# A two-branch attention layer on one core: exponentials of the second attention copied by ScalarE's queue into fp32r buffers and transposed there, over 15-row key ranges

## The chip, the cores and the metric

The kernel runs on one NeuronCore of a Trainium2 chip. The metric is device microseconds (us) from start to end of the program, the median of three runs. A profile of one further execution gives the start and duration of every instruction on the core's five engines: PE (TensorE; its weight loads are listed as PEld), DVE (VectorE), ACT (ScalarE), POOL (GpSimd) and SP (SyncE, which here issues almost all DMAs). Less than 0.2% (5 us) cannot be told from no change.

## The reference

Two sequences of 2048 tokens, width 1024, go through one layer with shared weights:

```
h = rms_norm(x)
q_a,k_a,v_a,g_a,q_b,k_b,v_b,g_b = split(h @ w_in)
A: 8 query heads, 2 key heads, keys within +-128 tokens, rotary, a learned sink per head
B: tokens as a grid of 32 rows x 64 columns; 8 heads; a query sees 8 rows x 16 columns of keys:
   rs = clip(row - 4, 0, 24);  cs = clip(col - 8, 0, 48)
   pr = softmax(q.k / 8 + relative position bias);  o = pr @ v
x = x + concat(o_a * silu(g_a), o_b * silu(g_b)) @ w_out
y = x + (p @ w_ple) * sigmoid(x @ w_ple_gate)
```

Everything is float32, head dimension 64. The second attention, B, is what the change touches.

## The kernel before, in words

**Arithmetic.** Matmul operands have the type fp32r, 4 bytes wide like fp32, which an engine that writes it rounds. To keep accuracy an operand is split in two fp32r parts, high (a cast on ACT) and low (the rest, by DVE or POOL), and a product takes three matmuls. Transposes go through PE too: the data is the stationary operand (it is loaded by LDWEIGHTS), an identity matrix of 128 columns streams past it, and the result appears in PSUM. They work on plain fp32 data with an fp32 identity (`ident`, or `rowwise`, which also permutes the tokens of a block).

**Stages.** Start: inputs and the first weights are loaded and split. Stage A (to about 780 us): projections of 32 blocks of 128 tokens (`proj_a`), with the first attention (`unit_a`) between their matmuls. Stage B (about 800 to 1815 us): projections for the second attention (`proj_b`; 24 matmuls `pqk` and 24 `pvg` per block and half of the heads), 64 of them, with 64 units of attention (`unit_b`) between. From about 1815 us on: the products with `w_out`, `w_ple_gate` and `w_ple` (a little of `w_ple` is done in the last units, `ple_ahead`).

**A unit of B.** A unit is one block of 8 x 16 queries and four heads. Its key window is `window(b, cb)`: `nr` rows of `ncol` columns, cut in chunks of `rows` rows, so that a chunk has at most 128 keys. The windows are 12 x 24, 12 x 32, 15 x 24 and 16 x 32 (rows x columns). The actions of a unit are:

- `sc(h)`, for h = 0 to 3: two matmuls into the PSUM tile `scb`; DVE adds the bias and takes the row maximum (`s`, `mx`).
- `exp`: ACT replaces each `s` by its exponentials, heads in the order 0, 2, 1, 3; the loads of the values `vw` are issued.
- `fin`, of the unit before (transposes `pgtb`), and `prep` (queries of the next unit, transposes `pqtb`).
- `pt(x)`: three or four transposes `ptb` of one head's exponentials; ACT and DVE split them into `p_t`.
- `po(x)`: three or four matmuls `pob` with the values; two by two they are added up by ACT and DVE (`otb`).

**What sets the order.** All PE instructions stand in the order in which the code gives them (`pinned`). `PLAN_B` says at which share of a unit's projection matmuls an action is put between them: a row (0.45, 1, "pt", 0) puts the first transposes of this unit behind 45% of them; a 0 in second place means the unit before. The other engines' instructions, and all DMAs, are ordered by a scheduler, except those that `P` keeps in the order of the code and those that `behind` ties to a matmul. Each queue is strictly in order, SP's and ACT's too. A DMA adds to one of eight completion counters (DMAHW0 to 7), taken in turn by all DMAs of SP and ACT, and waits until the DMA eight places before it has landed.

**Memory.** The 128 partitions' memory is given out by pools of tagged buffers. The tag `ev` has three buffers of 640 floats: in stage A for pairs of scores, at the end of stage B for results of `ple_ahead`; between, it is unused.

Of the kernel before, what the change touches and what calls it, by code (L numbers as in the profile page):

```python
# [11 lines left out]
F32 = mybir.dt.float32  # L12
F32R = mybir.dt.float32r
# [6 lines left out]
NT = SEQ // 128  # L20
# [2 lines left out]
NEG = -1.0e30  # L23
EPS = 1e-6

ROW_WIN = {0: (0, 12, 12), 1: (4, 16, 15), 2: (12, 16, 15), 3: (20, 12, 12)}
COL_WIN = {0: (0, 24), 1: (8, 32), 2: (24, 32), 3: (40, 24)}


def window(b, cb):  # L30
    c0, nc_ = COL_WIN[cb]
    r0, wide, narrow = ROW_WIN[b]
    nr = wide if nc_ == 32 else narrow
    rows = 5 if nr == 15 else 4
    return r0, nr, c0, nc_, rows


def row_type(b):
# [6 lines left out]

def query_rows(b, cb, j):

    r0, _, _, _, rows = window(b, cb)
    k0 = r0 + rows * j
    see = [r for r in range(8) if k0 - 7 <= min(max(8 * b + r - 4, 0), 24) <= k0 + rows - 1]  # L50
    return (see[0], max(see[-1] + 1, 4)) if see[0] == 0 else (min(see[0], 4), see[-1] + 1)


def bias_offsets():
# [28 lines left out]
TW = 512  # L83
# [10 lines left out]
PLAN_B = (  # L94
    (0.00, 1, "sc", 0), (0.03, 1, "sc", 1), (0.07, 1, "sc", 2), (0.09, 0, "po", 2), (0.11, 1, "sc", 3), (0.16, 0, "po", 3),
    (0.16, 1, "exp", 0), (0.24, 0, "fin", 0), (0.35, 1, "prep", 0),
    (0.45, 1, "pt", 0), (0.52, 1, "pt", 1), (0.60, 1, "pt", 2), (0.66, 1, "po", 0), (0.74, 1, "pt", 3), (0.80, 1, "po", 1),
)


def emit(ctx, tc, io):
# [6 lines left out]
        tag = PSM.get(tag, tag)  # L108
        return pp.tile(shape, F32, tag=tag, name=name, bufs=PSB[tag])

    ident = cp.tile([128, 128], F32, tag="ident", name="ident")
    make_identity(nc, ident)

    rowwise = cp.tile([128, 128], F32, tag="rowwise", name="rowwise")
    nc.gpsimd.tensor_copy(rowwise.rearrange("p (r c) -> p r c", c=16), ident.rearrange("p (c r) -> p r c", r=8))
    nw = cp.tile([128, KT], F32, tag="nw", name="nw")
    nc.scalar.dma_start(nw, io["norm_w"])
    ms_a = cp.tile([128, 2 * NT], F32, tag="ms_a", name="ms_a")
# [118 lines left out]
    def pinned(ins):  # L237

        if last_pe:
            tc.add_manual_dep(ins.ins, last_pe.pop().name,  # L240
                              mybir.DependencyInfo(mybir.DependencyClass.NoSync, mybir.DependencyReason.DATA),
                              reason="tensor engine order")
        last_pe.append(ins.ins)
# [8 lines left out]
        pinned(nc.tensor.matmul(out, lhsT, rhs, start=start, stop=stop))  # L252

    def tr(out, in_, eye=ident):
        pinned(nc.tensor.transpose(out, in_, eye))  # L255

    def project(ps, xr, w, cost):

# [16 lines left out]
    def exps(sm, fct, gs, sink=None):  # L275

        mx, nm, den, rd, ss = (sm[k] for k in ("mx", "nm", "den", "rd", "s"))
        if sink is None:
            nc.vector.tensor_scalar_mul(nm, mx, -1.0)  # L279
            yield  # L280
        else:
            nc.vector.scalar_tensor_tensor(out=nm, in0=mx, scalar=-1.0, in1=sink[1], op0=ALU.mult, op1=ALU.min)
        for n_, i in enumerate((0, 2, 1, 3) if sink is None else range(4)):
            ex = nc.scalar.activation(ss[i], ss[i], AF.Exp, bias=nm[:, i:i + 1], accum_out=den[:, i:i + 1])  # L284
# [374 lines left out]
        qrest[f] = split_q(pqt, q1, q2, 1)  # L659
        return q1, q2  # L660

    p_rot = []

    def unit_a(f, kv):
        s, t = divmod(f, NT)
# [5 lines left out]
        def sc(i):  # L671
            pair, half = divmod(i, 2)
            a, z = span[half]
            c0, n = 128 * t - 128 + 64 * half, z - a
            if half == 0:
                pairs.append(ap.tile([128, 640], F32, tag="ev", name="s2", bufs=3))
# [168 lines left out]
    def unit_b(f):  # L845
# [2 lines left out]
        b, cb = divmod(j, 4)  # L848
        _, gs = held[f]
        r0, nr, c0, ncol, rows = window(b, cb)  # L850
        kc, nch = rows * ncol, nr // rows
        n = nr * ncol
        if cb != 2:
            off, _ = BIAS_OFF[(row_type(b), col_type(cb))]
# [7 lines left out]
        def load_values():  # L862

            spare = f >= 6 * NT - 6 and f % 2 == 0
            if spare:
                four = ap.tile([128, 4, 4, 2 * HD], F32R, tag="raw", name="vw4", bufs=1)
            for j in range(nch):
                v = four[:, j] if spare else \
                    ap.tile([128, 4, 2 * HD], F32R, tag=("vp", "vr_")[j % 2], name="vw", bufs=3 - j % 2)
                nc.sync.dma_start(v[:kc].bitcast(F32).rearrange("p h d -> p (h d)"),  # L870
                                  v_d[half, s, cb][r0 + rows * j:r0 + rows * j + rows]
                                  .rearrange("r c h a d -> (r c) (h a d)"))
                vw.append(v)

# [5 lines left out]
        def sc(h):  # L880
            ps = ptile([128, 512], "sc", "scb")
            for j, q in enumerate(qs[f]):
                mm(ps[:, :n].rearrange("p (r c) -> p r c", c=ncol), q[h % 2][:, 128 * (h // 2):128 * (h // 2) + 128],
                   ks_b[h % 2][:, r0:r0 + nr, h // 2, c0:c0 + ncol], j == 0, j == 1)
            softmax(h, ps, n, bias[:, h, :n], sm)
            if h == 3:
                got["ex"] = exps(sm, hr_b[:, st:st + 1], gs)
                next(got["ex"])

        def pt(x):  # L890
            h = (0, 2, 1, 3)[x]
            pt = ptile([128, 512], "pt", "ptb")
            for j in order:

                c = at[j] - 16 * sees[j][0]
                tr(pt[:kc, c:c + 128], sm["s"][h][:, kc * j:kc * j + kc], rowwise)
# [3 lines left out]
            nc.vector.tensor_tensor(out=lo, in0=pf, in1=hi.bitcast(F32), op=ALU.subtract)  # L900
            p_ts.append(p_t)

        def po(x):
            h = (0, 2, 1, 3)[x]
            e, i = h % 2, h // 2
            if i == 0:
                got["po"] = ptile([128, 2, 256], "ms", "pob")
            if x == 0:
                got["ot"] = ap.tile([128, 2, 2, 128], F32, tag="ot", name="otb", bufs=2)
            po, ot = got["po"], got["ot"]  # L910
            for j in order[::-1]:
                a, z = sees[j]
                mm(po[:, i, :].rearrange("p (a q) -> p a q", a=2)[:, :, 16 * a:16 * z], vw[j][:kc, h, :],
                   p_ts[x][:kc, :, at[j]:at[j + 1]], j == order[-1], j == order[0])
            if i == 1:
                a, z = 64 * e, 64 - 64 * e
                pq = po.rearrange("p i (a q) -> p i a q", a=2)
                nc.scalar.copy(ot[a:a + 64], pq[z:z + 64])  # L918
                nc.vector.tensor_tensor(out=ot[a:a + 64], in0=pq[a:a + 64], in1=ot[a:a + 64], op=ALU.add)  # L919
# [58 lines left out]
            early[name].append(w)  # L978
        del coming[:n]

    made = []

    def store_ple(n):

# [4 lines left out]
    def ple_ahead(n, tail=False):  # L989

        load_p(n + 1)
        for m in range(KT):
# [11 lines left out]
            if tail:  # L1004
                ev = main.tile([128, TW], F32, tag="s", name="ev", bufs=SB)
            else:
                ev = ap.tile([128, TW], F32, tag=("ev", "sq")[m // 2 % 2], name="ev", bufs=3 - m // 2 % 2)
            P(nc.scalar.copy(ev, ps))
            store_ple(1)
            if tail:  # L1010
# [416 lines left out]
```

## Time and profile before

| | |
|---|---|
| Three runs, us | 2465.88, 2467.28, 2467.45; median 2467.28 |
| Span of the profiled execution, first to last instruction, us | 2462.8 |
| Busy, share of the span | PE 100%, PEld 84%, DVE 69%, ACT 57%, POOL 35% |
| Granted TensorE clock | 1.000 of full speed |
| DMA traffic | 442.01 MB, 179 GB/s on average |

The profiled execution is a run of its own; the page gives its span, which is 4.5 us under the median of the three runs. Its time outside the span is not listed, so those 4.5 us are taken as what lies around the span.

How to read it: PE counts as busy whenever a matmul is in its pipeline, and matmuls overlap there, so 100% says that PE is always occupied, not that it runs at its best rate. The rate is seen in the chain that ended last, which gives each piece the time by which it delays the next. In lists of groups, "128*96 128x128" behind a PE instruction means 128 rows by 96 columns of stationary data, and 128 columns that stream past.

### The profile page before, as it was taken

To read this page: it belongs to the slowest core of one execution; us is meant where nothing else is said; L and a number is where in the kernel's file an instruction comes from. 1 tells how busy PE (TensorE), PEld (TensorE's weight loads), DVE (VectorE), ACT (ScalarE), POOL (GpSimd) and SP (SyncE) were. 2 spreads that over 40 slices of the span, in tenths; PEclk is the share of its full clock that TensorE was granted. 3 is DMA by queue.
4 is the path that set the end of the run, shared out by engine and by line. 5 is a ranking of instruction groups with operands and counts; after the bars stand their busy time and mean duration, and the time that the engine had idled before them with its cause. 6 is when DMAs were issued, how large, how long until landed. Compare 5 with 4: busy or idle time off the path is not lost.

```text
span 2462.8 us, 40532 instructions
## 1 busy us (share of the span) xinstructions
PE 2451.7 (100%) x13062; PEld 2075.4 (84%) x13062; DVE 1704.7 (69%) x4214; ACT 1413.1 (57%) x3408; POOL 856.8 (35%) x1363
## 2 busy tenths in 40 slices
PE   9999999999999999999999999999999999999999
PEld 8888888888888888888888888888888888888887
DVE  7777777777765666666666666666537655677776
ACT  6777776777664665656655566665763222344433
POOL 4555555555543544454444444443100000000000
PEclk9999999999999999999999999999999999999999
DMA  6332223332255565556955566667977445856765
GB/s 228 123 103 93 95 89 103 95 101 88 95 180 166 167 192 182 183 163 195 314 187 183 170 219 202 193 199 242 317 248 262 154 165 178 270 180 206 251 222 171
DMA packets 243316, 442.01 MB, mean 179 GB/s; under 512 B 27904, under 2 KB 82592, under 8 KB 237856
## 3 DMA queue, kind: packets, MB, share of 16 engines
q1 hardware_dynamic: 242816, 439.42, 54.8%
q8 instruction: 104, 1.70, 0.3%
q14 instruction: 108, 0.88, 0.1%
q10 hardware_dynamic: 288, 0.01, 0.0%
HBM read 309.29 MB, written 134.23 MB: 180 GB/s over the span
## 4 chain that ended last, share of the span: by engine, by line
PE 94%; DVE 2%; ACT 2%; POOL 1%; issue 1%; DMA 1%; SPq 0%; ACTq 0%; POOLq 0%; DVEq 0%
PE pvg L252 15%; PE pqk L252 14%; PE acca L1230 14%; PE accc L1230 11%; PE pg L252 6%; PE pq L252 6%; PE scb L252 4%; PE ptb L255 4%; PE pple L252 4%; PE pob L252 3%; PE po L252 3%; PE pk L252 3%; PE sc L252 3%; PE pt L255 2%; DVE pr L712 1%
## 5 line engine op out<-in xcount | busy, mean ns | idle before, releaser
L284 ACT ACTIVATE s<-s,nm 128x320 f32<-128x320 f32 (+6 forms) x512 | 294.5, 576 | 318.5 <-DVE nm L279 198.9
L252 PE MATMUL pvg<-wb,xr 128*128 128x512 f32 x1536 | 461.5, 407 | 0.0
L252 PE MATMUL pqk<-wa,xr 128*128 128x512 f32 x1536 | 442.9, 411 | 0.0
L252 PEld LDWEIGHTS pqk<-wa,xr 128*128 128x128 f32 x1536 | 266.1, 189 | 36.7
L252 PEld LDWEIGHTS pvg<-wb,xr 128*128 128x128 f32 x1536 | 266.8, 189 | 30.8
L1212 ACT CAST opd<-raw 128x512 fp32r<-128x512 f32 x224 | 131.5, 618 | 271.7 <-PE acca L1230 118.0
L353 POOL TENSOR_TENSOR xr<-stx,xr 128x512 fp32r<-128x512 f32 x186 | 238.9, 1295 | 101.3 <-ACT xr L352 76.8
L1213 DVE TENSOR_TENSOR opd<-raw,opd 128x512 fp32r<-128x512 f32 x224 | 146.7, 687 | 146.9 <-ACT opd L1212 146.9
L252 PE MATMUL pg<-wb,xr 128*128 128x512 f32 x768 | 233.3, 410 | 1.0 <-DVE vv L510 1.0
L252 PE MATMUL pq<-wa,xr 128*128 128x512 f32 x768 | 219.3, 400 | 0.0
L268 DVE CUSTOM_DVE_ANT_0 s<-scb,bias 128x288 f32<-128x288 f32 (+3 forms) x256 | 142.2, 556 | 104.6 <-PE scb L252 101.7
L137 POOL TENSOR_TENSOR yb<-vrb,power 128x8 f32<-128x8 f32 x64 | 106.4, 1662 | 222.1 <-DVE vrb L784 202.4
L1230 PE MATMUL accc<-opd,wb 128*128 128x512 f32 x768 | 176.7, 389 | 0.0
L1230 PE MATMUL acca<-opd,wa 128*128 128x512 f32 (+1 forms) x780 | 175.9, 386 | 0.5 <-ACT r L1308 0.5
L1230 PE MATMUL acca<-opd,s 128*128 128x512 f32 x768 | 175.4, 389 | 0.0
L1230 PEld LDWEIGHTS acca<-opd,wa 128*128 128x128 f32 x780 | 145.0, 188 | 30.2 <-ACT r L1308 0.7
L1230 PEld LDWEIGHTS acca<-opd,s 128*128 128x128 f32 x768 | 144.2, 188 | 29.9
L1230 PEld LDWEIGHTS accc<-opd,wb 128*128 128x128 f32 x768 | 144.2, 188 | 29.9
L919 DVE TENSOR_TENSOR otb<-pob,otb 64x512 f32<-64x512 f32 x128 | 88.1, 688 | 113.2 <-ACT otb L918 111.5
L252 PEld LDWEIGHTS pob<-p_t,vw 128*128 128x128 f32 (+2 forms) x832 | 132.6, 189 | 23.4 <-DVE p_t L900 3.4
L252 PEld LDWEIGHTS pq<-wa,xr 128*128 128x128 f32 x768 | 135.2, 189 | 17.3
L712 DVE TENSOR_TENSOR pr<-pt,pr 128x512 fp32r<-128x512 f32 (+2 forms) x248 | 135.4, 549 | 15.9 <-ACT pr L710 12.5
(171 smaller groups left out, 5169.9 us busy)
## 6 DMA issues: line engine op xcount, KB each, us to landing
stx<-x_b SPq DMA_DIRECT2D x128, 256.0 KB
vw<-v_d SPq DMA_DIRECT2D x112, 256.0 KB
stx<-x_a SPq DMA_DIRECT2D x64, 256.0 KB
stn<-x_n SPq DMA_DIRECT2D x64, 256.0 KB
v_d<-vb SPq DMA_DIRECT2D x64, 256.0 KB
ple_d<-ev SPq DMA_DIRECT2D x64, 256.0 KB
xres<-x_r SPq DMA_DIRECT2D x64, 256.0 KB
x_d<-r SPq DMA_DIRECT2D x64, 256.0 KB
```

The source lines that it names most:

```text
L137: nc.gpsimd.tensor_tensor(out=y, in0=v, in1=power.broadcast_to([128, n]), op=ALU.pow)
L252: pinned(nc.tensor.matmul(out, lhsT, rhs, start=start, stop=stop))
L255: pinned(nc.tensor.transpose(out, in_, eye))
L268: nc.vector.tensor_tensor_reduce(out=s, in0=ps[:, :n], in1=bias, scale=1.0, scalar=-3.0e38, op0=ALU.add, op1=ALU.max, accum_out=sm["mx"][: ...
L284: ex = nc.scalar.activation(ss[i], ss[i], AF.Exp, bias=nm[:, i:i + 1], accum_out=den[:, i:i + 1])
L353: low.tensor_tensor(out=lo, in0=raw, in1=hi.bitcast(F32), op=ALU.subtract)
L712: nc.vector.tensor_tensor(out=pr[r, 1, to], in0=pt[r, c], in1=pr[r, 0, to].bitcast(F32), op=ALU.subtract)
L919: nc.vector.tensor_tensor(out=ot[a:a + 64], in0=pq[a:a + 64], in1=ot[a:a + 64], op=ALU.add)
L1212: P(nc.scalar.copy(hi, v))
L1213: P(nc.vector.tensor_tensor(out=lo, in0=v, in1=hi.bitcast(F32), op=ALU.subtract))
L1230: pinned(nc.tensor.matmul(ps[:, cols], w[k][:, a, c:c + 128], o[:, b, cols], start=i in (0, 1, 4) and k == 0 and j == 0, stop=k == 3 and j ...
```

## The change

Four things, all of which concern stage B, its buffers or its identities:

1. **Key ranges.** The windows of 16 x 32 become 15 x 32 (8 query rows see no more than 15 key rows), in chunks of 4, 4, 3 and 4 rows (`chunks`). The chunk of three rows is still transposed over 128 columns; the last 32 are not used.
2. **Copies.** In units 32 to 89 of the running number `f` (58 of the 64 units of B) each head's exponentials are copied by a DMA that ACT's queue issues from `s` to a slot of a new tile `tn`, of four slots of 480 fp32r numbers, bit for bit. The transposes read `tn`; they run as fp32r, with identities of that type. The last six units transpose the fp32 data as before. The DMAs stand between the exponentials: ex0, ex2, copy 0, ex1, copy 2, ex3, copy 1, copy 3; all of these now keep the code's order.
3. **Buffers.** `ev` becomes one buffer of 3 x 640 numbers, in turn cut in three for `unit_a`, held as `tn`, and cut in three for `ple_ahead`. `ident` and `rowwise` become fp32r; the fp32 matrix that they are made from lies in a pool `eye` that is closed before the pool `main` is opened, so that tiles of `main` can lie in its place.
4. **Plan.** `pt` and `po` of the same unit move back by 0.04 to 0.06 of a unit.

```diff
-ROW_WIN = {0: (0, 12, 12), 1: (4, 16, 15), 2: (12, 16, 15), 3: (20, 12, 12)}
+ROW_WIN = {0: (0, 12), 1: (4, 15), 2: (12, 15), 3: (20, 12)}
...
+    rows = 5 if nr == 15 and nc_ == 24 else 4
...
+def chunks(nr, rows):
+
+    first = list(range(0, nr - rows, rows)) + [nr - rows]
+    return [(k, min(rows, z - k)) for k, z in zip(first, first[1:] + [nr])]
...
-    (0.45, 1, "pt", 0), (0.52, 1, "pt", 1), (0.60, 1, "pt", 2), (0.66, 1, "po", 0), (0.74, 1, "pt", 3), (0.80, 1, "po", 1),
+    (0.51, 1, "pt", 0), (0.58, 1, "pt", 1), (0.65, 1, "pt", 2), (0.72, 1, "po", 0), (0.78, 1, "pt", 3), (0.84, 1, "po", 1),
...
+    ident, rowwise = (cp.tile([128, 128], F32R, tag=n, name=n) for n in ("ident", "rowwise"))
+    with tc.tile_pool(name="eye", bufs=1) as ep:
+        eye_ = ep.tile([128, 128], F32, tag="eye", name="eye")
+        make_identity(nc, eye_)
+        nc.vector.tensor_copy(ident, eye_)
+        nc.gpsimd.tensor_copy(rowwise.rearrange("p (r c) -> p r c", c=16), eye_.rearrange("p (c r) -> p r c", r=8))
...
     def tr(out, in_, eye=ident):
-        pinned(nc.tensor.transpose(out, in_, eye))
+        if in_.dtype == F32R:
+            pinned(nc.tensor.transpose(out.bitcast(F32R), in_, eye))
+        else:
+            pinned(nc.tensor.transpose(out, in_, eye.bitcast(F32)))
...
+        waiting = []
         for n_, i in enumerate((0, 2, 1, 3) if sink is None else range(4)):
             ex = nc.scalar.activation(ss[i], ss[i], AF.Exp, bias=nm[:, i:i + 1], accum_out=den[:, i:i + 1])
-            if sink is None and n_ == 0:
+            if sink is None and (n_ == 0 or turned is not None):
                 P(ex)
+            if sink is None and turned is not None:
+                waiting.append(i)
+                for k in waiting[:1] if n_ in (1, 2) else waiting[:] if n_ == 3 else ():
+                    to = turned[:, k, :ss[k].shape[-1]]
+                    P(nc.scalar.dma_start(to.bitcast(F32), ss[k]))
+                    ss[k] = to
+                    waiting.remove(k)
...
-                got["ex"] = exps(sm, hr_b[:, st:st + 1], gs)
+                if not tn:
+                    tn.append(ap.tile([128, 4, 480], F32R, tag="ev", name="tn", bufs=1))
+                got["ex"] = exps(sm, hr_b[:, st:st + 1], gs, turned=tn[0] if f < 6 * NT - AHEAD - 1 else None)
```

What the scheduler makes of it is seen at three places. First SP's queue at the start of the program. `stx` are the inputs, `ws` with 2x256 columns the weights of the first product, `ws` with 2x512 and `wg` weights that are needed later. Before:

```order
L335 DMA stx<-x_a 128x512
L232 DMA ws<-w_in 128x2x256
L335 DMA stx<-x_a 128x512
L232 DMA ws<-w_in 128x2x256 x3
L335 DMA stx<-x_a 128x512 [waits DMAHW0_49]
L335 DMA stx<-x_a 128x512 [waits DMAHW1_49]
L232 DMA ws<-w_in 128x2x512 [waits DMAHW2_49]
```

After:

```order
L238 DMA ws<-w_in 128x2x512 x2
L238 DMA wg<-w_in 128x512 x4
L424 DMA rw<-rope_w 128x64 [waits DMAHW0_49]
L446 DMA snk_all<-sink 128x8 [waits DMAHW1_49]
L352 DMA stx<-x_a 128x512 [waits DMAHW2_49,DVE_49,Pool_49]
L238 DMA ws<-w_in 128x2x256 [waits DMAHW3_49]
L352 DMA stx<-x_a 128x512 [waits DMAHW4_49]
L238 DMA ws<-w_in 128x2x256 [waits DMAHW5_49]
L238 DMA ws<-w_in 128x2x256 [waits DMAHW6_49]
L238 DMA ws<-w_in 128x2x256 [waits DMAHW7_49]
```

The first `stx` now waits for the copies of the identity on DVE and POOL, and six loads of later weights, 2 MB, have moved ahead of it.

Second, ACT's queue in a unit with a window of 15 x 24. Before:

```order
L779 ACTIVATE sqb<-pqk 128x512 [waits PE_49]
L284 ACTIVATE s,den<-s,nm 128x360 [waits DVE_49]
L918 COPY otb<-pob 64x512 [waits PE_49]
L284 ACTIVATE s,den<-s,nm 128x360 x3
L837 ACTIVATE q1b<-pqtb,wk 64x256 [waits PE_49]
```

After:

```order
L799 ACTIVATE sqb<-pqk 128x512 [waits PE_49]
L942 COPY otb<-pob 64x512 [waits PE_49]
L294 ACTIVATE s,den<-s,nm 128x360 [waits DVE_49]
L294 ACTIVATE s,den<-s,nm 128x360 [waits DMAHW4_49]
L301 DMA tn<-s 128x360 [waits DMAHW2_49,DMAHW0_49,Activation_49]
L294 ACTIVATE s,den<-s,nm 128x360
L301 DMA tn<-s 128x360 [waits DMAHW2_49,Activation_49]
L294 ACTIVATE s,den<-s,nm 128x360 [waits DMAHW6_49]
L301 DMA tn<-s 128x360 [waits DMAHW3_49,Activation_49]
L301 DMA tn<-s 128x360 [waits DMAHW7_49,DMAHW4_49,Activation_49]
L857 ACTIVATE q1b<-pqtb,wk 64x256 [waits PE_49]
```

The copy `otb`, which stood behind the first exponential, now stands ahead of it, and the four DMAs stand between the exponentials and behind them, each waiting for the exponential that it reads and for DMA counters.

Third, PE's queue around the first transposes of a unit, `pt(0)`. `pktb` are transposes of the block's keys. Before:

```order
L255 MATMUL pqtb<-ident,qg 128x128
L252 MATMUL pvg<-wb_9843,xr 128x512
L252 MATMUL pvg<-wb_9845,xr 128x512 x3
L252 MATMUL pvg<-wb_9847,xr 128x512
L255 MATMUL ptb<-rowwise,s 120x128 [waits DVE_49,Activation_49]
L255 MATMUL ptb<-rowwise,s 120x128 x2
L252 MATMUL pvg<-wb_9847,xr 128x512 x2
L255 MATMUL pktb<-ident,kb 128x128 [waits DVE_49,PE_49]
```

After:

```order
L264 MATMUL pqtb<-ident,qg 128x128
L258 MATMUL pvg<-wb_9730,xr 128x512
L258 MATMUL pvg<-wb_9732,xr 128x512 x3
L258 MATMUL pvg<-wb_9734,xr 128x512 x3
L264 MATMUL pktb<-ident,kb 128x128 [waits DVE_49,Activation_49]
L264 MATMUL pktb<-ident,kb 128x128
L258 MATMUL pqk<-wa_9501,xr 128x512
L262 MATMUL ptb<-rowwise,tn 120x128 [waits DMAHW0_49]
L262 MATMUL ptb<-rowwise,tn 120x128 x2
```

`pt(0)` has moved behind three more matmuls of 512 columns and the two `pktb`, and waits for the landing of a DMA in place of ACT.

More of the change, by code (lines that the diff above doesn't have):

```diff
@@ L31, in window @@
     c0, nc_ = COL_WIN[cb]
-    r0, wide, narrow = ROW_WIN[b]
-    nr = wide if nc_ == 32 else narrow
-    rows = 5 if nr == 15 else 4
+    r0, nr = ROW_WIN[b]
+    rows = 5 if nr == 15 and nc_ == 24 else 4
     return r0, nr, c0, nc_, rows
+def chunks(nr, rows):
+    first = list(range(0, nr - rows, rows)) + [nr - rows]
+    return [(k, min(rows, z - k)) for k, z in zip(first, first[1:] + [nr])]
 def row_type(b):
@@ L46, in query_rows @@
 def query_rows(b, cb, j):
-    r0, _, _, _, rows = window(b, cb)
-    k0 = r0 + rows * j
-    see = [r for r in range(8) if k0 - 7 <= min(max(8 * b + r - 4, 0), 24) <= k0 + rows - 1]
+    r0, nr, _, _, rows = window(b, cb)
+    k, n = chunks(nr, rows)[j]
+    see = [r for r in range(8) if r0 + k - 7 <= min(max(8 * b + r - 4, 0), 24) <= r0 + k + n - 1]
     return (see[0], max(see[-1] + 1, 4)) if see[0] == 0 else (min(see[0], 4), see[-1] + 1)
@@ L675, in sc @@
             if half == 0:
-                pairs.append(ap.tile([128, 640], F32, tag="ev", name="s2", bufs=3))
+                if not s2:
+                    s2.extend([ap.tile([128, 3, 640], F32, tag="ev", name="s2", bufs=1), 0])
+                pairs.append(s2[0][:, s2[1] % 3])
+                s2[1] += 1
                 if not right:
@@ L850, in unit_b @@
         r0, nr, c0, ncol, rows = window(b, cb)
-        kc, nch = rows * ncol, nr // rows
+        kc, ch = rows * ncol, chunks(nr, rows)
+        nch, kn = len(ch), [ncol * n for _, n in ch]
         n = nr * ncol
@@ L869, in load_values @@
                     ap.tile([128, 4, 2 * HD], F32R, tag=("vp", "vr_")[j % 2], name="vw", bufs=3 - j % 2)
-                nc.sync.dma_start(v[:kc].bitcast(F32).rearrange("p h d -> p (h d)"),
-                                  v_d[half, s, cb][r0 + rows * j:r0 + rows * j + rows]
+                nc.sync.dma_start(v[:kn[j]].bitcast(F32).rearrange("p h d -> p (h d)"),
+                                  v_d[half, s, cb][r0 + ch[j][0]:r0 + sum(ch[j])]
                                   .rearrange("r c h a d -> (r c) (h a d)"))
@@ L979, in load_coming @@
         del coming[:n]
-    made = []
+    made, evs = [], []
     def store_ple(n):
@@ L1006, in ple_ahead @@
             else:
-                ev = ap.tile([128, TW], F32, tag=("ev", "sq")[m // 2 % 2], name="ev", bufs=3 - m // 2 % 2)
+                if not evs:
+                    evs.extend([ap.tile([128, 3, 640], F32, tag="ev", name="ev", bufs=1), 0])
+                if m // 2 % 2:
+                    ev = ap.tile([128, TW], F32, tag="sq", name="ev", bufs=2)
+                else:
+                    ev = evs[0][:, evs[1] % 3, :TW]
+                    evs[1] += 1
             P(nc.scalar.copy(ev, ps))
```

15 lines of the change are left out of this document (6 added, 9 removed).

## The prediction, made before the changed kernel ran

> **What bounds the kernel now.** I read the page's busy shares first, then the chain of work that ended last over the 58 units that get copies (about 805 to 1740 us), then single units in that chain, then the groups of weight loads.
>
> ```profile
> span 2462.8 us, 40532 instructions
> PE 2451.7 (100%) x13062; PEld 2075.4 (84%) x13062; DVE 1704.7 (69%) x4214; ACT 1413.1 (57%) x3408; POOL 856.8 (35%) x1363
> by line: PE pvg L252 34.6%; PE pqk L252 34.5%; PE scb L252 9.0%; PE ptb L255 8.8%; PE pob L252 8.2%; PE pktb L255 1.4%; PE pgtb L255 1.4%; PE pqtb L255 1.3%; PE pple L252 0.9%
> 1200.00:1400.00 200.00, 200.00 (x1089) 168.40 (x1088) 131.64 (x338) 121.02 (x287) 97.32 (x110) 1.00 0.66 212
> 1600.00:1740.00 140.00, 140.00 (x759) 117.42 (x758) 95.45 (x238) 86.24 (x200) 50.71 (x61) 1.00 0.72 231
> ```
>
> The third line is the chain by line: it is PE from end to end, so in these units only what PE spends per instruction counts. The last two are windows (PE, PEld, DVE, ACT, POOL busy, granted clock, DMA share, GB/s): PE is never idle, the clock is full, ACT and DVE have 35 to 40% to spare, and the DMA engines are busy for 0.66 to 0.72. The transposes `ptb` take 8.8% of 935 us, 82 us; the list of one tile finds 753 of them there:
>
> ```profile
> L255 PE MATMUL ptb<-rowwise,s x753: 270/272/275, 805.7 to 1730.8; 128*128 128x128 f32 x102, 128*120 128x128 f32 x45, 128*96 128x128 f32 x42
> ```
>
> The 272 ns are not a cost: they are the time in the pipeline, and 82 us / 753 = 109 ns is what one costs.
>
> **The transposes.** Pieces of the chain in a unit of 12 x 24 (the first five lines) and of one of 16 x 32 (the last four):
>
> ```profile
> 1319.94 1.16 PE pvg L252 x5
> 1321.10 0.33 PE ptb L255 x3
> 1321.43 0.46 PE pvg L252 x2
> 1321.89 0.22 PE pktb L255 x2
> 1322.11 0.23 PE pqk L252
> ...
> 1392.56 0.47 PE scb L252 x2
> 1400.67 0.44 PE ptb L255 x4
> 1404.54 0.40 PE pob L252 x4
> 1404.94 0.98 PE pqk L252 x4
> ```
>
> A transpose costs 0.33/3 = 110 ns with 96 stationary columns and 0.44/4 = 110 ns with 128. A cost that doesn't go with the stationary columns is not the load; it is the 128 fp32 columns that stream past. As fp32r they should stream faster: a piece of 96 dense fp32r matmuls gives 21.76/96 = 227 ns per 512 columns, 57 ns per 128.
>
> ```profile
> 1913.58 21.76 PE acca L1230 x96
> L255 PEld LDWEIGHTS ptb<-rowwise,s 128*128 128x128 f32 x448 | 56.7, 140 | 15.6
> L255 PEld LDWEIGHTS ptb<-rowwise,s 128*96 128x96 f32 x192 | 23.1, 126 | 8.6 <-ACT s L284 0.2
> L255 PEld LDWEIGHTS pms<-ident,ms_a 128*16 128x16 f32 x2 | 0.2, 88 | 0.1
> L252 PEld LDWEIGHTS pob<-p_t,vw 128*128 128x128 f32 x448 | 70.1, 189 | 11.4 <-DVE p_t L900 0.8 <-ACT xr L352 0.5
> ```
>
> Then the load of the next stationary block may bind instead. For transposes it takes 140, 126 and 88 ns at 128, 96 and 16 columns, about 0.46 ns a column, so some 60 ns of it grow with the columns (62 with the slope between 96 and 16). An ordinary fp32r load (`pob`) is 49 ns longer, some 110 ns. No transpose of fp32r is in this trace, so its price has two ends: 57 ns (the stream binds), and 117 ns, which the narrowest fp32r matmuls cost: the four `pob` above stream 128 to 256 columns and take 0.40 us, and the `pqk` behind them, 0.98 in place of 0.91 for four, give 0.07 more; 0.47/4. I take 62: a transposing load is nearest to what the new instruction does. 756 transposes change: 756 x (62 - 110) = **-36.3 us**. It is all on the path.
>
> One rule of the notes speaks against this. The Trainium skill, "TensorE: Matmul & The Clock Gate", section "LDWEIGHTS (loading the stationary operand)", gives a load the time of its columns divided by 1.2 per ns, 107 ns for 128 columns. With that for the new transposes hardly anything is gained on 110 ns, and the time would be that of the first rival. The transposing loads of this trace grow by 0.44 ns a column between 96 and 128, about half of what the rule has; `pob`'s loads fit it.
>
> **Fifteen rows.** 128 `scb` matmuls have 480 columns in place of 512. By the chain, the pair of 512 takes 0.47 us, 0.235 each, 0.45 ns a column: 128 x 32 x 0.45 = **-1.8 us**. The number of transposes and of `pob` stays. Bias, maxima and exponentials get 6% narrower in half of the units; that's on ACT and DVE, which have time. At most these edits give the 1.8 us and nothing more.
>
> **The start.** The inputs `stx` now wait for the identity's copies and stand behind 2 MB of later weights on SP's queue. Before, these were the rows:
>
> ```profile
> 0.72 0.39 SPq L335 DMA_DIRECT2D stx<-x_a  x1
> 3.74 0.62 ACT L352 CAST xr<-stx 128x512 fp32r<-128x512 f32 x1 [0.81 <-DMA stx<-x_a]
> 5.36 7.87 PE L252 MATMUL pk<-wx,xr 128*128 128x256 f32 x47
> 11.08 2.07 ACT L151 ACTIVATE wa<-ws,nw 128x512 fp32r<-128x512 f32 x3 [0.78 <-DMA ws<-w_in]
> ```
>
> Between the first landing, at 3.74, and that of the first `ws` of 2 x 512, at 11.08, seven loads of 256 KB and one of 512 KB came in: 2.25 MB (of 2^20 bytes) in 7.34 us. Two MB ahead cost 2 x 3.26 = **+6.5 us**: the first `pk` starts at about 12 in place of 5.36. PE works on from there to the end, so nothing hides it. Ends: +4, if `pk`, paced by loads before (7.87 us for 48 matmuls of 256 columns, where 48 x 114 ns = 5.5 would do), runs densely now; +8 with the 1.5 us that the identity's copies and the next waits may add.
>
> **The copies.** 58 x 4 DMAs of 128 x 288 to 480 numbers, 45 MB. On ACT an issue held the queue for 0.40 to 0.47 us:
>
> ```profile
> 0.72 0.40 ACTq L117 DMA_DIRECT2D nw<-norm_w  x1
> 1.15 0.47 ACTq L125 DMA_DIRECT2D wkt<-qk_norms  x1
> ACT s L284 <- DVE nm L279: 190.1, 57, 4.1
> 1317.36 0.54 ACT L284 ACTIVATE s<-s,nm 128x288 f32<-128x288 f32 x1 [2.91 <-DVE nm L279]
> 1318.01 0.58 ACT L918 COPY otb<-pob 64x512 f32<-64x512 f32 x1
> ```
>
> ACT sits idle 190 us over 57 units ahead of the exponentials, 3.3 us each, so 4 x 0.45 = 1.8 us of issues fit if they come late; they stand, however, before `q1b` and the next splits. Those are covered by the shift of the plan: `pt` and `po` of a unit keep their distances, and the splits of the next `p_t` come an action later. Cost: nothing, as long as `pt(0)` isn't late. The copies add 45 MB/935 us = 48 GB/s to 212, or 0.15 to the DMA share: 0.81, and 0.88 in the last window, where little is free any more.
>
> What can be late is the landing. `pt(0)` used to wait for an exponential; now it waits for a DMA behind that. The plan moves it behind two `pvg`, two `pktb` and a `pqk`, 0.46 + 0.22 + 0.23 = 0.91 us by the chain: to 1322.0 in this unit. `otb` now goes first on ACT: it can start at about 1317.45, as `pob` ends, the first exponential at 1318.03, and the copy is issued when that ends with its sum, near 1318.8. That leaves 3.2 us. How long a DMA takes from issue to landing is seen in these rows:
>
> ```profile
> 0.72 3.18 DMA nw<-norm_w
> 36.55 0.94 SPq L335 DMA_DIRECT2D stx<-x_a  x2
> 39.32 0.62 ACT L352 CAST xr<-stx 128x512 fp32r<-128x512 f32 x1 [1.61 <-DMA stx<-x_a]
> 664.89 4.30 DMA pre<-w_in
> ```
>
> 3.18 us for 4 KB on ACT's queue, 39.32 - 36.55 = 2.77 us and 4.30 us for 256 KB on SP's. I take 3.35, the mean of 3.18 and of the middle of the other two: 0.15 us late, in each of 58 units, **+9 us**. Ends: 0 (2.77) and 1.1 us a unit (4.30), 64 us. The other heads' copies follow each other by half a microsecond and their transposes by 1.25 us, so they have more slack. Each copy also waits for the DMA eight places before it, of SP or of ACT; at 1.2 us for each of SP's 256 KB (212 GB/s) those lie several us back. Should SP hold one of them back for a full buffer, ACT stands still with it: this counts under the late landing.
>
> The Trainium skill, "DMA: Bandwidth & Descriptors", has 2.0 us plus the bytes at 436 GB/s for a DMA, from its own runs of another queue kind: by estimate 2.5 us for a copy, no stall, and a sum of 2436. The rows above are all longer than that.
>
> **Sum.** Against the profiled span: 2462.8 - 36.3 - 1.8 + 6.5 + 9 = 2440.2. The median of the runs before is 2467.28, 4.5 us over that span; with those, **2445 us**. A change within 0.2% (5 us) is what a measurement of this kernel can't tell from none; 2445 is 0.9% under 2467. The edits break even where (6.5 - 1.8 + 9)/756 = 18 ns are gained, at 92 ns a transpose.
>
> **Rivals.**
> - *The fp32r load binds (other side).* A load of type fp32r costs what `pob`'s do, 49 ns over the transposing fp32 load, and a transpose stays at 110 to 117 ns. For it: every fp32r load in the trace has 188 or 189 ns, and narrow fp32r matmuls cost 117. Against it: none of them is a transpose, and the loads of fp32 transposes, of the same 4 bytes, are short. Then 2462.8 + 6.5 - 1.8 + 9 + 4.5 = 2481, with 117 ns 2486; without a late landing 2472. It decides from 92 ns on. Chance 0.31.
> - *Half of it.* Stream and load don't overlap fully, and the price is some 85 ns: -18.9 in place of -36.3, 2462. For it: no narrow matmul here reaches the dense 57 ns. Chance 0.15.
> - *The landing is late.* 4.30 us or a held queue, 1.1 us per unit in which PE waits at `pt(0)`: 2445 + 55 = 2500. For it: the DMA share goes to 0.8 and more. Against: most of the rows are shorter. Chance 0.07.
> - *The main case*, 57 to 75 ns and 0 to 0.4 us late: chance 0.47, its own range 2430 to 2457. Its lower end: 756 x 53 ns = 40 gained, no stall, +4 at the start: 2430.
>
> **Range and chances.** The likeliest case gives 2445. The range goes from 2430 to 2484: below lie some 6%, above the late landing and the worst of the first rival, some 12%. Faster by over 0.2%: the main case with 0.46, half of the partial one (0.07) and a little of the first rival with no stall and a cheap start, 0.02: 0.55. Within 0.2%: the rest of the partial price and the first rival without stalls, 0.12. Slower: 0.33.
>
> **What would show it.** Right: in the chain `ptb x3` goes from 0.33 to about 0.19 and `x4` from 0.44 to 0.25; the loads of `ptb` stay near 140 ns; the first `pk` starts near 12; the idle time of PE before `ptb` is put down to the DMA of `tn` with under 20 us in all. Loads of 189 ns and an unchanged `x3` of 0.33 would show the first rival; 60 us of waits for `tn`, or ACT waiting for DMA counters, the third. What would make the prediction wrong otherwise: a start that costs far more than the loads ahead of it, and PE losing more in the first attention, where `ev` is now shared.

## The result, and the profile after

The changed kernel took 2652.15 us (median of 4 runs, 2650.66 to 2653.01) against 2466.58 us of the kernel before, run beside it: a ratio of 1.0753, 95% interval 1.074 to 1.0765. It is 7.5% slower, where 0.9% faster was forecast; the time lies far above the range.

The page of the profiled execution (span, then busy time by engine), and one window of the second attention (PE, PEld, DVE, ACT, POOL busy, granted clock, DMA share, GB/s):

```profile
span 2651.2 us, 40912 instructions
PE 2502.4 (94%) x13062; PEld 2095.0 (79%) x13062; DVE 1704.9 (64%) x4215; ACT 1411.8 (53%) x3408; POOL 849.7 (32%) x1363
1200.00:1400.00 200.00, 179.14 (x929) 146.07 (x928) 111.58 (x283) 99.61 (x233) 80.59 (x91) 0.95 0.68 229
```

PE was busy for all of these 200 us before; now it stands still for 21 of them, and its granted clock is 0.95 in the mean where it was 1.00. The loss lies almost whole in the 58 units with copies. The first scores of the second attention start at 807.7 us (798.1 before: the start costs 9.6 us); from there to the first unit without copies it takes 1113.7 us in place of 936.1, +177.6; the rest of the program takes 1.3 us more.

The wait of PE for the copies in that stretch (who waits for whom: us in all, times, longest), and the chain through one unit of 12 x 32:

```profile
PE ptb L262 <- DMA tn<-s: 120.8, 68, 4.7
...
1760.53 0.74 ACT s L294 x3
1761.27 6.86 DMA tn<-s
1768.12 0.04 issue
1768.17 0.62 PE ptb L262 x3
1768.79 1.41 PE pqk L258 x3
1770.20 0.34 PE ptb L262 x3
1770.54 1.83 PE pqk L258 x4
```

Two things are to be seen. The copy takes 6.86 us from its issue to its landing, and PE waits. And when PE goes on, its `pqk` cost 1.41/3 = 0.47 and 1.83/4 = 0.46 us each, where they cost 0.23 before: PE runs at half clock. In the clock records, this stretch holds 25 pieces of 3.4 or 6.8 us at 0.5, 119 us together; the kernel before has none there. PE is busy for 108 of these 119 us; at full clock that work would take half as long, so the half clock costs at most 54 us.

DMA issues of that unit, and of the one before it, 17 us earlier (issue start, time on the queue, queue):

```profile
1742.57 1.28 SPq L891 DMA_DIRECT2D vw<-v_d  x3
1744.09 0.47 ACTq L301 DMA_DIRECT2D tn<-s  x1
1747.43 0.45 PE L262 MATMUL ptb<-rowwise,tn 128*128 128x128 f32 x3
...
1759.74 1.28 SPq L891 DMA_DIRECT2D vw<-v_d  x3
1761.11 0.38 SPq L879 DMA_DIRECT2D bias<-bias  x1
1761.27 0.47 ACTq L301 DMA_DIRECT2D tn<-s  x1
```

In the first the copy has three loads of values ahead of it, and the transposes start 3.34 us after its issue, almost without a wait. In the second a load of the next unit's bias (576 to 960 KB) was issued 0.16 us ahead of it, and the landing takes twice as long. Over the 58 units, the first copy lands after a mean of 4.1 us in the 17 that have no bias load issued around it, and 5.5 us in the other 41; all copies have a median of 5.5 us.

Windows over the two landings and over the stretch behind the second (columns as above) show what the copies meet:

```profile
1744.09:1747.40 3.31, 3.28 (x17) 2.39 (x15) 1.11 (x4) 2.37 (x8) 1.66 (x3) 1.00 0.98 352
1761.27:1768.10 6.83, 3.26 (x17) 2.37 (x15) 3.99 (x9) 4.29 (x11) 2.44 (x5) 0.90 0.94 289
1768.17:1773.59 5.42, 5.42 (x19) 4.33 (x20) 1.11 (x3) 2.29 (x6) 0.00 (x0) 0.50 0.55 211
```

While a copy is under way, the DMA engines are busy for 0.98 and 0.94 of the time, although their share over 200 us is 0.68: the loads come in a burst, and the copy is issued into it. Over all 58 first copies the share is 0.97 between issue and landing. The third line has the clock at 0.50 with PE busy throughout.

The start, on SP and PE:

```profile
0.73 0.96 SPq L238 DMA_DIRECT2D ws<-w_in  x2
1.73 2.21 SPq L238 DMA_DIRECT2D wg<-w_in  x4
5.43 0.35 SPq L352 DMA_DIRECT2D stx<-x_a  x1
12.72 0.55 PE L258 MATMUL pk<-wx,xr 128*128 128x256 f32 x1 [7.47 <-issue]
```

The first input is issued at 5.43 in place of 0.72, and the first `pk` starts at 12.72 in place of 5.36.

### The profile page after: what moved, and what is told of

Read it like the earlier page. It is cut to its first block, busy times and chain, and to the rows that moved or that the text cites. A ratio compares the mean times of both kernels' runs of the same rounds, so it can differ in the third digit from the quotient of the medians.

```text
span 2651.2 us, 40912 instructions
## 1 busy us (share of the span) xinstructions
PE 2502.4 (94%) x13062; PEld 2095.0 (79%) x13062; DVE 1704.9 (64%) x4215; ACT 1411.8 (53%) x3408; POOL 849.7 (32%) x1363
## 5 line engine op out<-in xcount | busy, mean ns | idle before, releaser
L258 PE MATMUL pqk<-wa,xr 128*128 128x512 f32 x1536 | 492.5, 440 | 0.0
L258 PE MATMUL pvg<-wb,xr 128*128 128x512 f32 x1536 | 447.1, 404 | 0.0
L258 PEld LDWEIGHTS pqk<-wa,xr 128*128 128x128 f32 x1536 | 283.4, 204 | 36.3
L262 PEld LDWEIGHTS ptb<-rowwise,tn 128*128 128x128 f32 (+2 forms) x756 | 91.9, 149 | 176.1 <-DMA tn<-s 138.2
L262 PE MATMUL ptb<-rowwise,tn 128*128 128x128 f32 (+2 forms) x756 | 104.1, 257 | 121.0 <-DMA tn<-s 120.8
L924 DVE TENSOR_TENSOR p_t<-ptb,p_t 128x368 fp32r<-128x368 f32 (+5 forms) x256 | 119.7, 486 | 130.3 <-ACT p_t L923 129.3
L923 ACT CAST p_t<-ptb 128x368 fp32r<-128x368 f32 (+5 forms) x256 | 106.3, 425 | 177.5 <-PE ptb L262 152.4
L942 ACT COPY otb<-pob 64x512 f32<-64x512 f32 x128 | 74.3, 581 | 225.0 <-PE pob L258 224.7
```

What stands on the lines that cost most here:

```text
L262: pinned(nc.tensor.transpose(out.bitcast(F32R), in_, eye))
```

## The experiments

Four theories were to be told apart: late landing (with the half clock behind it), the price of an fp32r transpose, the plan's shift, and the start. Each diff below is against the changed kernel unless it says otherwise.

**Without copies.**

```diff
-got["ex"] = exps(..., turned=tn[0] if f < 6 * NT - AHEAD - 1 else None)
+got["ex"] = exps(..., turned=None)
```

> The changed kernel without the copies: the transposes read the fp32 exponentials as before; key ranges, plan, buffers and start stay as changed. Theory 1 (the copies land late, PE stands still at the first transposes of a unit and then runs some us at half clock): the loss in the second attention goes away whole, and what is left is the later start, +9.6 us in the changed trace at the first scores of the second attention, less 1.8 us for fifteen rows: about 2474 us. Rival A (the shifted plan or the shared buffer is at fault): it stays above 2500. Rival B (the start costs nothing in the end): 2465.

Measured: 2521.88 us, 1.0224 (1.0209 to 1.0239). This missed theory 1, and lies where rival A had it. Without the copies, 130 of the 186 us are gone, but the time is 48 us over the one expected:

```profile
PE pob L258 <- DVE p_t L924: 35.1, 46, 1.6
```

PE now waits at the products `po` for the splits of the transposed exponentials.

**Copies that nothing reads.**

```diff
-                    ss[k] = to
```

> The copies are issued and land as in the changed kernel, but nothing reads them; the transposes read the fp32 exponentials. Theory 1 (only the wait for the landing hurts): as without copies, about 2474 us, with the landing still at a median of 4 to 5.5 us from the issue. Rival C (the 232 issues on ACT's queue, its waits for DMA counters, or the 45 MB of traffic hold up the other work): a good part of the loss stays, 2520 to 2650 us.

Measured: 2527.58 us, 1.0242 (1.0225 to 1.026), 6 us over the run without copies, with the copies landing at a median of 5.4 us. The number lies in the range of rival C, but only because the 48 us are here as well. Against the run without copies, the issues on ACT's queue and the 45 MB cost little; it is the wait for the landing that costs. ACT isn't untouched, though: PE's waits at `po`, 41 us in place of 35, are now mostly for work of ACT:

```profile
PE pob L258 <- ACT qg L839: 18.5, 16, 2.4
PE pob L258 <- ACT xr L368: 9.7, 12, 1.2
```

**Written as fp32r.**

```diff
-ex = nc.scalar.activation(ss[i], ss[i], AF.Exp, ...)
+ex = nc.scalar.activation(turned[:, i, :n], ss[i], AF.Exp, ...)   # no dma_start
```

> ACT writes the exponentials straight into the fp32r buffers (rounded to that type, which changes the values slightly); no DMA copies, and the transposes read fp32r. This measures the price of an fp32r transpose alone, against the run without copies (110 ns each). At the 62 ns that the prediction took, 36 us less than that run: about 2438 us. At the 93 ns that the changed trace shows where PE doesn't wait, 756 x 17 ns = 13 us less: about 2461 us. At 110 ns, no gain: 2474 us.

Measured: 2476.03 us, 1.0038 (1.0025 to 1.0051). By its sum that would be the third case, no gain. It can't be read so: the scheduler ordered ACT and DVE differently here, and the waits at `po` are 12.1 us, not 35.1. The price had to be taken from a run with the old plan (below).

**The plan alone.** The kernel before, with nothing but the shares of `pt` and `po` changed:

```diff
-    (0.45, 1, "pt", 0), (0.52, 1, "pt", 1), (0.60, 1, "pt", 2), (0.66, 1, "po", 0), ...
+    (0.51, 1, "pt", 0), (0.58, 1, "pt", 1), (0.65, 1, "pt", 2), (0.72, 1, "po", 0), ...
```

> The kernel before with nothing changed but the shares of the plan (pt and po of a unit 0.04 to 0.06 later). Theory 2 (the scheduler then puts the splits p_t on ACT and DVE behind those of vb, ks_b and qg, and PE waits at po; 37 us of gaps in the run without copies): 2500 to 2515 us, with gaps of 30 to 40 us before pob. Rival (the loss of the run without copies comes from its buffers or key ranges): 2467 us.

Measured: 2512.32 us, 1.0185 (1.017 to 1.02), 46 us over the kernel before. The chain of a unit shows the mechanism:

```profile
PE pob L252 <- DVE p_t L900: 33.8, 43, 1.7
...
1302.63 0.64 DVE ks_b L756
1303.27 0.02 issue
1303.29 0.63 ACT ks_b L755
1303.92 0.02 issue
1303.94 0.61 DVE ks_b L756
1304.56 0.03 issue
1304.59 0.49 DVE p_t L900
1305.07 0.04 issue
1305.12 0.56 PE pob L252 x3
...
1307.45 0.29 PE pob L252 x3
```

The splits of the keys, `ks_b`, stand ahead of the split `p_t` on both engines. In the kernel before, ACT has one `p_t` ahead of the first `ks_b` and another ahead of the second:

```profile
1323.15 0.42 ACT L899 CAST p_t<-ptb 96x320 fp32r<-96x320 f32 x1
...
1323.97 0.60 ACT L755 CAST ks_b<-pktb 64x256 fp32r<-64x256 f32 x1
...
1324.90 0.41 ACT L899 CAST p_t<-ptb 96x320 fp32r<-96x320 f32 x1
...
1325.71 0.63 ACT L755 CAST ks_b<-pktb 64x256 fp32r<-64x256 f32 x1
```

With the transposes only 0.06 of a unit later the scheduler puts `vb`, both `ks_b` and `qg` ahead of them all, and PE stands at `po`. The distances from `pt` to `po`, on which the prediction relied, hardly change in the plan for `po(0)` and `po(1)` (0.21 of a unit as before, and 0.26 in place of 0.28); the queues behind it do. The plan leaves `po(2)` and `po(3)` where they are in the next unit, so these do come nearer to their `pt`, by 0.05 and 0.04.

This run also shows what a stop of PE costs besides its idle time. Its 58 units take 42.4 us more than those of the kernel before, at full clock throughout, but PE is idle for only 31.9 us, in 44 stops: 0.24 us a stop are not counted as idle. The chain has them behind the stop, where three `pob` take 0.56 us in place of 0.29.

**The upper bound.** Exponentials written as fp32r, no copies, the plan's old shares, and `ident` left in fp32, so that nothing holds up the start:

```diff
+    ident, rowwise = (cp.tile([128, 128], t, ...) for n, t in (("ident", F32), ("rowwise", F32R)))
+    make_identity(nc, ident)
+    nc.gpsimd.tensor_copy(rowwise..., ident...)          # no pool "eye"
```

> The upper bound of the idea: exponentials written by ACT in fp32r straight into the buffers (rounded to that type), no copies, the plan's old shares, the start repaired, fifteen rows. If the plan's shift and the start are the only losses beside the copies, the kernel before less 756 x 17 ns and 1.8 us: 2452 us, with the splits p_t waiting no more than before. If an fp32r transpose really cost 62 ns: 2429 us. If the gain is eaten by another wait: 2460 us or more.

Measured: 2451.78 us, 0.9944 (0.9932 to 0.9957), 14.2 us under the kernel before. The stretch of 58 units takes 919.8 us in place of 936.1. Its chain, in a unit of 12 x 24 (three rows) and one of 15 x 32 (the rest), and its loads:

```profile
1377.10 0.20 PE ptb L259 x3
1378.30 0.20 PE ptb L259 x3
1378.50 0.77 PE pqk L255 x3
...
1383.91 0.45 PE scb L255 x2
1394.48 0.30 PE ptb L259 x4
1394.78 0.76 PE pqk L255 x3
L259 PEld LDWEIGHTS ptb<-rowwise,tn 128*128 128x128 f32 x408 | 47.8, 141 | 13.6
```

The piece of three is 0.20 in place of 0.33, nearly the 0.19 forecast. But the three `pqk` behind it take 0.76 or 0.77 where they took 0.69 or 0.70: part of the transposes' time shows up there. (0.20 + 0.07)/3 = 90 and (0.30 + 0.07)/4 = 92 ns. Taken from start to start over all units, with what the following product takes longer, it is 92.5 ns with 128 stationary columns, 90 with 120 and 83 with 96: 17, 20 and 27 ns less than before. 408 x 17 + 180 x 20 + 168 x 27 = 15.1 us, and with 1.7 us for the rows 16.8; the two stretches differ by 16.3, and the time at `pob` is 0.8 us longer. The load is still 141 ns long, as for fp32 (140). The pair of `scb` goes from 0.47 to 0.45.

**The start alone.** The same edit to the identities, and nothing else:

> The changed kernel with ident left in fp32 and only rowwise copied to fp32r, so that no extra pool holds up the inputs: SP's first loads are those of the kernel before. The start theory: the first pk returns to about 5.4 us, the first scores of the second attention to 798 us, and the whole is 9 to 10 us shorter than the changed kernel: about 2643 us. Rival (the later start is absorbed or re-made by the long stage behind it): 2652 us.

Measured: 2651.61 us, 1.0745 (1.072 to 1.0771); its runs lie between 2641.59 and 2657.41, too far apart to see 9 us. In its trace the first `pk` starts at 5.21 and the second attention at 799.8, 8 us earlier than in the changed kernel; its 58 units then took 1123.0 us in place of 1113.7, with 123.5 us of waits and 140 us at half clock. So the start's 8 us are shown, and that they reach the end is not.

**Loads behind the copies.** An action `val` at 0.36 of a unit issues the unit's values and the next unit's bias, each tied to a product:

```diff
-"exp": lambda _: (next(got["ex"]), load_values())
+"exp": lambda _: next(got["ex"]),
+"val": lambda _: (load_values(), load_bias(f + 1) if f + 1 < 6 * NT else None)
```

> The changed kernel, but SP's loads of the values and of the next unit's bias are given behind the copies (at 0.36 of a unit, each tied to a product) in place of just ahead of them. Theory 1a (the copies land late because 1 to 2 MB of loads have been issued within 2 us before them): the copies land in 3.1 to 3.6 us from the issue, PE waits under 0.5 us a unit, and the time is 2465 to 2485 us. Rival D (a copy between two places of the core's memory takes 5 us whatever else is under way): the landing stays at 4 to 6 us and the time above 2600 us.

Measured: 2608.54 us, 1.0571 (1.0555 to 1.0587). The total missed by far; the copies land even earlier than expected. The first of a unit takes 2.0 to 2.3 us in 49 of the 58 units (median of all copies 2.9), which rules out rival D, and `pt` waits in few units:

```profile
PE pob L258 <- DMA vw<-v_d: 40.0, 59, 1.8
PE pob L258 <- DVE p_t L935: 20.2, 18, 2.0
PE ptb L262 <- DMA tn<-s: 16.7, 9, 4.3
```

The waits for the copies went from 120.8 us to 16.7. What took their place is a wait for the values at `po`, since these are now the loads that come late, and 51 us are still at half clock. The Trainium skill, "DMA: Bandwidth & Descriptors", section "Anatomy of one DMA — SWDGE (gpsimd) path", gives a DMA (measured on another kind of queue) 2.0 us and the bytes at 436 GB/s, by estimate 2.3 to 2.6 us for these copies: the quiet copies agree with it to a few tenths, the crowded ones take twice as long and more.

**The same with the start repaired and the plan's old shares.**

> All three repairs: the start of the run before this one in the list, the loads of values and bias behind the copies, and the plan's old shares (pt(0) at 0.45), with which the splits p_t stand ahead of those of vb and ks_b again. By theories 1 and 2 together: copies land in 2.1 us where pt(0) leaves them about 2.3, gaps under 20 us in all, and against the kernel before 756 transposes at 93 ns in place of 110 (-13 us) and fifteen rows (-2 us) remain: 2452 to 2470 us. If the price of the copies lies elsewhere (ACT's queue, traffic), 2500 us or more.

Measured: 2665.14 us, 1.0795 (1.0769 to 1.0821), a miss by 200 us. The first copies land in 2.0 to 2.3 us in 48 units, but `po` is 0.06 of a unit earlier, and the values are later still:

```profile
PE pob L255 <- DMA vw<-v_d: 64.0, 81, 3.8
PE ptb L259 <- DMA tn<-s: 23.9, 10, 5.3
```

With these stops 116 us of the 58 units are at half clock, about as much as in the changed kernel. The expectation had costed the moved loads at nothing.

**Only the bias behind the copies.** `load_values()` stays in `exp`:

> The changed kernel with one thing moved: the next unit's bias is loaded behind the copies. Start, plan and the values' loads as changed. Theory 1: units without a bias load show copies that land in 3.1 to 4.2 us where pt(0) leaves them 3.2, so PE's wait at pt falls from 121 us to 20 to 45 us, the half clock from 119 us of time to under 40, and the whole to 2540 to 2590 us. Rival (bias loads only mark the units that are late anyway): within 20 us of 2652.

Measured: 2576.27 us, 1.0445 (1.0429 to 1.0461), in the range expected. PE's wait for the copies:

```profile
PE ptb L262 <- DMA tn<-s: 63.8, 63, 3.6
```

It fell from 120.8 us, less than expected, and 48 us are at half clock. Copies have a median of 4.1 us. So the bias loads make about half of the wait. That the values' loads make the rest fits the two runs in which both were moved, where the first copies land in 2.1 us; no run moves the values alone.

**Only later.** Loads where the changed kernel has them; `pt` and `po` later by 0.20 to 0.14 of a unit:

```diff
-    (0.51, 1, "pt", 0), (0.58, 1, "pt", 1), (0.65, 1, "pt", 2), (0.72, 1, "po", 0), (0.78, 1, "pt", 3), (0.84, 1, "po", 1),
+    (0.71, 1, "pt", 0), (0.77, 1, "pt", 1), (0.83, 1, "pt", 2), (0.88, 1, "po", 0), (0.92, 1, "pt", 3), (0.98, 1, "po", 1),
```

> The changed kernel with the transposes and products of a unit at 0.71 to 0.98 of it in place of 0.51 to 0.84; loads and copies stay where they are. pt(0) then has some 6.4 us from the issue of its copy in place of 3.2. Theory 1 (late landing): the landing stays at a median of 5 to 5.5 us, but only the latest of the copies (up to 8 us) still hold PE; the waits at pt go from 121 us to under 30, the half clock mostly goes with them, 2490 to 2540 us. Rival (each stall is only pushed on to the products po, whose splits come later too): above 2580 us.

Measured: 2533.61 us, 1.027 (1.0247 to 1.0293). The copies land at a median of 5.8 us and pt(0) comes 5.4 us after the issue (not 6.4, as expected); the waits are a third, where under 30 us were expected:

```profile
PE ptb L262 <- DMA tn<-s: 39.9, 44, 1.9
PE pob L258 <- DVE p_t L924: 3.6, 5, 1.4
```

`po` waits for splits only 3.6 us here, although `ks_b` and `qg` stand ahead of `p_t`: with the transposes this late those are mostly done by then.

**Start repaired, later, bias behind the copies.**

> Copies as in the changed kernel, with the start repaired, pt and po of a unit at 0.71 to 0.98, and the next unit's bias loaded behind the copies; the values' loads stay ahead of them. In the run with the later plan alone, PE waited at pt only in units with a bias load under way. Theory 1 (late landing, of which the bias is the worse half): the copies land in 3 to 4.5 us, pt(0) leaves them 5.4, PE waits under 5 us in all at pt, no half clock, and 13 us of cheaper transposes and 2 us of rows remain less what splits still wait: 2450 to 2475 us. If the copies' DMAs cost something besides their landing, 2490 us or more.

Measured: 2479.38 us, 1.0055 (1.0042 to 1.0067). This is 4 us over the range that was expected. The copies land at a median of 4.5 us and the waits for them are nearly gone:

```profile
PE ptb L259 <- DMA tn<-s: 7.3, 14, 1.1
PE pob L255 <- DVE p_t L932: 4.3, 5, 1.5
```

It took 173 us off the changed kernel with the copies left in, and is still 13 us over the kernel before. Its stretch of 58 units takes 941.8 us, 22 us more than the upper bound. PE is idle for 16 us of it (most of the two rows above, and a few waits at the scores and in the units with `ple_ahead`), in 24 stops; at the 0.24 us a stop of the run with the plan alone, these add 6 us by estimate.

**Later still**, pt(0) at 0.74 and the bias at 0.48:

> The run with repaired start, later plan and moved bias, with the transposes another 0.03 of a unit later (pt(0) at 0.74, po(1) at 0.99) and the bias load at 0.48 in place of 0.36. There, 16 waits of pt for late copies and a few of po were left, and the second attention took 22 us more than with no copies. Theory 1: with half a microsecond more, and the bias clear of the last copies too, those waits shrink to a few, and the time is 2458 to 2472 us, near the kernel before or just under it. If what is left comes from the copies' traffic or from ACT's queue, it stays at 2475 to 2485 us.

Measured: 2475.76 us, 1.0038 (1.0024 to 1.0051); waits for copies 5.6 us. The time cannot be told from that of the run before it, and lies where the other case of the expectation put it, the copies' traffic or ACT's queue. Its 58 units take 941.3 us, 21.5 more than the upper bound; 15.1 are idle time of PE, and 24 stops at 0.24 us make 6 more by estimate. So the loss still sits in stops and not in slower work, but most of them are no longer waits for copies: 9.5 of the 15.1 us are waits for splits, scores and `ple_ahead`. Why those come later than without copies was not isolated. No version with copies beat the kernel before, and the 14 us of the upper bound were got only by writing rounded exponentials.

## Why the prediction was wrong

**The landing** is the step that failed most. The slack was worked out as 3.2 us, and the trace has 3.1 to 3.3 in the units where PE doesn't wait. The landing was put at 3.35 us with 4.30 at most; the copies measured 3.2 to 7.9 (5th to 95th of a hundred), 5.5 in the middle. The term of +9 us was 120.8 us of waits, twice its upper end. The first copies have 0.6 to 1.4 MB of loads issued within the 2 us ahead of them, because `exp` issues the values at the same moment; the runs with moved loads (2.1 us) show that this is the cause. Of the rows that the estimate came from, the short ones had at most 0.25 MB ahead, and only the one of 4.30 us had 0.75 MB: it was the row most like the copies, and it was taken as the far end. The DMA share that the prediction went by, 0.66 to 0.88, is a mean that hides the burst (0.97 while the first copies are under way). The plan names the loads in the same action as the exponentials, so it could have been seen. The third rival had the mechanism, but its price of 1.1 us a unit and 2500 us were too small.

**The half clock** had no term at all. To the 177.6 us add the 16.3 that were gained, and take off 128 us of gaps in PE, 121 at `ptb` and 7 at `pob`: some 66 are left. The half clock can make up to 54 of them, so at least 12 are something else. The 86 stops at 0.24 us each make 21 by estimate, which leaves some 45 for the half clock. This share is argued from the clock records and the run with the plan alone, and not isolated by a run.

**The plan's shift** was costed at nothing, "as long as `pt(0)` isn't late". By itself it costs 46 us. In the changed kernel only 7 us of waits at `pob` are left of it, presumably since PE's stops at `pt` give the splits their time: the two losses overlap and must not be added.

**The transposes** were put at 62 ns, and are 83 to 92.5. The step at fault is the use of the load's slope for the whole price. (By its own rows that slope gives 61; and the 110 ns of an ordinary load that were said to go with its columns are inferred, since every such load in the trace has 128 columns and 189 ns.) Between two transposes in a row the trace does have 61 to 67 ns; what was missed is the change from the last of them to the next product. The prediction had added what shows in the following `pqk` to `pob`'s piece, and did not for the transposes that it forecast; with those 0.07 us its own 62 would have been 80 to 85. The first rival (a long load, 110 to 117 ns) is wrong too: the load is 141 ns and not 189. It is nearest to "half of it", 85 ns. Its break-even of 92 ns, with its own other terms, would have meant no gain.

**The start** was +6.5 and measured +9.6, over its upper end of +8: the first `pk` came at 12.72 as forecast (about 12), but 2 us more were lost between it and the second attention. **The rows** gave 1.7 us of their 1.8. That **ACT's queue** has room for the issues was right as far as the sum goes: unread copies cost 6 us. The feared loss in the first attention, where `ev` is shared, did not come: with the start repaired the upper bound reaches the second attention at 798.8 us, against 798.1.

## What to carry to other kernels

Take a DMA's latency from the moment at which it will be issued, with what the other queue issues there, and not from quiet rows of the trace or from a mean DMA share; a DMA in a dependency that an engine used to fill needs slack for the crowded case, and the bulk loads moved out of its way come late themselves. On a PE that never idles, a stop of 2 us costs more than 2 us: here 0.24 us at each stop, and more where the clock halved behind it. Where a scheduler orders the other queues, a shift of a few hundredths in one engine's plan is a change of its own: run it alone before anything is built on it.

## What the runs showed of the hardware

In these traces the clock falls on a grid. All pieces at half clock in the changed kernel's trace start at the same phase of a period of 3.413 us (2.08 us into it), to 4 ns, and those of the 58 units last one or two periods; other runs have another phase. From full clock, a period with PE idle for under 0.46 of it was never followed by one at half here, and from 0.56 on it always was (25 switches, between 0.46 and 0.92; in the run with the bias moved 13, from 0.51 on). The lower edge is not fixed: with loads behind the copies and the old plan, idle shares from 0.35 on led to half clock. From 0.56 on every run looked at switched, so about 1.9 us without matmuls in one period were enough. Behind a period at half clock, 0.07 to 0.41 of it idle held the clock at half for another in ten cases. The Trainium skill, "TensorE: Matmul & The Clock Gate", section "Why this matters for your kernels", advises to have no idle gaps over about 3 us between bursts; here shorter ones did it, such as one of 2.0 us that lay whole in one period, and one of 3.4 us that was split over two did not.

Copies inside the core's memory of 144 to 240 KB landed at a median of 2.2 us after their issue where no load had been issued in the 2 us before (133 copies of the run with loads behind them), and at a median of 6.6 us, up to 8.5, behind 0.7 to 1.6 MB of loads on another queue (the changed kernel). An fp32r transpose takes 83 ns with 96 stationary columns, 90 with 120 and 92.5 with 128, an fp32 one 110 with any of them; so in fp32r the price goes a little with the columns loaded.
